# Merging the block inverses of the four DeltaNet heads in lockstep: four visits of small matmuls instead of sixteen

## The chip, the cores and the metric

The kernel runs on one core of a Trainium2 chip. The metric is the device time of one execution in microseconds (us). The engines of a core work side by side, each through its own instructions in order: TensorE (PE, matmuls, with the weight load PEld in front of each), VectorE (DVE), ScalarE (ACT), GpSimd (POOL), and SyncE (SP), which issues DMAs.

## The reference

One layer of a decoder trunk, sequence 1024, width 1024, float32. One input projection feeds two mixers: a gated DeltaNet with 4 heads of 128 (causal convolution on q, k and v, normalised q and k, chunked delta rule) and a dilated sliding-window attention with 8 heads of 64. Both outputs go through one output projection and a residual; a gated MLP with a short convolution, another residual and a norm follow. The part that is touched is the triangular solve of the delta rule:

```python
lmat = dec_strict * kk * bc[..., None, :]
rhs = jnp.concatenate([vc, gam * kc], axis=-1)
sol = lax.linalg.triangular_solve(lmat, rhs, left_side=True, lower=True, unit_diagonal=True)
u_v, w_k = sol[..., :Dv], sol[..., Dv:]
```

## The kernel before

**The solve.** The kernel works with chunks of 128 tokens, so 8 chunks for each of 4 heads, and inverts the 128x128 unit triangular matrix of each. `kprep` builds the matrices of a head (tile um) and parks their diagonal 32x32 blocks in DRAM. When all heads are there, `forward_sub` (line 663) inverts all diagonal blocks of 32x32 (4 for each chunk and head) on VectorE, in 31 steps over all blocks at once, and parks the inverses and their transposes (xdram, xtdram). `merge` (line 698) then puts larger inverses together from smaller ones: for a lower triangular matrix in 2x2 blocks, the block below the diagonal of the inverse is minus (one inverse) times (the block) times (the other inverse), so two products. From 32 to 64 these are the products into w1p and y1p (32x32 matmuls), from 64 to 128 those into w2p and y2p (64x64). Between two products the result is copied from PSUM to SBUF by ACT and DVE. Each matmul on float32 stands in the trace as two instructions.

**Before, pair by pair.** `merge` is a generator and runs once for each pair of heads, as a stream of its own (line 688). Each of the four products is cut into a part for each head (`for e in range(2)`), and `apart` (line 693) keeps the parts at least MGAP = 0.6 us from each other on the planner's clock, so that projection products stand between them: 2 pairs x 4 products x 2 heads = 16 visits. Pair 0 uses the PSUM tag "asc", pair 1 "ch", each with two banks.

**What sets the order.** The class `Weave` runs generators ("streams") with a level each; `wv.need(...)` gives the planned time at which a tile is ready, and a stream yields until then, with a slack (MSLACK = 1.5 us for the merges). The last argument of `mm` is what a matmul costs on the planner's clock of TensorE. Line 191 stamps every matmul with its place, so TensorE's order is the planner's. The order on the other engines is made by the framework's scheduler; the instructions of the recurrence go through `uv` and `ua`, which raise their priority.

**What stands around.** `dense` (line 505) is the stream of the lowest priority: 25 column tiles of the projection, each 2 x 24 products of 128x128 by 128x512 (tiles xhi, xlo, whi, wlo: three products for each of 8 slices of the width). Each half of 24 has a PSUM bank ("hf", two of them), which DVE evacuates (`scaled`, tile xr or aqkv). At each column tile the weights of the next one but one are loaded (wst), and those of the next are split by ACT (whi) and DVE (wlo). `chain` (line 791) is the recurrence over 8 chunks, once for each head; it begins when all four heads are merged (`wv.until(("m", i))`). One chunk takes the products ct,kT, then r,um, then wke,ktok, then ct,qat and w,qat, with DVE and ACT between them (r, wke, w, ct, vtok). Its tiles qat come by DMA from parked tensors; the loads for the second half of heads 0 and 1 use the same two slots ("go") as the tiles x64. The attention follows when the chains are done.

Of the kernel before, what the change touches and what calls it, by code (L numbers as in the profile page):

```python
# [7 lines left out]
F32 = mybir.dt.float32  # L8
F32R = mybir.dt.float32r
AF = mybir.ActivationFunctionType  # L10
OP = mybir.AluOpType
# [4 lines left out]
P = 128  # L16
S = 1024
KT = 8
H = 4
NCH = 8  # L20
# [16 lines left out]
MSLACK = 1.5  # L37
# [3 lines left out]
MGAP = 0.6  # L41
# [103 lines left out]
def hybrid_layer(tc, I, out):  # L145
    nc = tc.nc
    wv = Weave()
    ve = Engine(wv, nc.vector, "vector", 0.07, 0.00105)
    ac = Engine(wv, nc.scalar, "scalar", 0.12, 0.00085)
# [3 lines left out]
    po_ = Engine(wv, nc.gpsimd, "gpsimd", 0.15, 0.0021)  # L153
    sy = Engine(wv, nc.sync, "sync", 0.05, 0.00142, 2.2)
# [6 lines left out]
    sp = es.enter_context(tc.tile_pool(name="sp", bufs=1))  # L161
# [3 lines left out]
    def tile_(pool, shape, dt, name, tag, bufs):  # L165
        return wv.slot(pool.tile(list(shape), dt, name=name, tag=tag, bufs=bufs), tag, bufs)
# [20 lines left out]
    def after(inst, anchor, reason="keeps a slot free until it is needed"):  # L187
        tc.add_manual_dep(inst.ins, anchor.ins.name, order, reason=reason)

    def mm(dst, lhs, rhs, us, start=True, stop=True, **kw):  # L190
        tc.stamp_issue_order_token(nc.tensor.matmul(dst, lhs, rhs, start=start, stop=stop, **kw).ins, TOKEN)  # L191
        wv.product(us, dst, lhs, rhs)
# [52 lines left out]
    xdram = dp.tile([H, 32, 1024], F32, name="xdram")  # L245
    xtdram = dp.tile([H, 32, 1024], F32, name="xtdram")
# [6 lines left out]
    def bank(tag, name="ps"):  # L253
        return tile_(pp_, (P, 512), F32, name, tag, 2)
# [239 lines left out]
    G = [dict() for _ in range(H)]  # L494
# [82 lines left out]
    def kprep(h):  # L577
# [50 lines left out]
        if all(("k", i) in wv.done for i in range(H)):  # L628
            forward_sub()
# [33 lines left out]
    def forward_sub():  # L663

        mt_t = A("mt", "go")
        sy.dma_start(mt_t, mdram.rearrange("h p f -> (h p) f"))
        mt = mt_t.rearrange("p (j i) -> p j i", j=32)
        xi_t = A("xi", "go")
        xi = xi_t.rearrange("p (i c) -> p i c", i=32)
        tmp = tile_(sp, [P, 256], F32, "tmp", "t1", 1)  # L670
        po_.memset(xi, 0.0)
        po_.affine_select(xi, xi, pattern=[[1, 32], [-1, 32]], compare_op=OP.not_equal, fill=1.0, base=0,
                                channel_multiplier=0)

# [12 lines left out]
        for p in range(2):  # L687
            wv.add(2, merge(p, anchor))

    mlast = [0.0]  # L690
    mark = const("mark", [P, 1])

    def apart():

        while wv.pe < mlast[0] + MGAP:
            yield mlast[0] + MGAP - wv.pe

    def merge(pair, anchor):

        tag = ("asc", "ch")[pair]  # L700
        yield wv.need(xdram)
        hs2 = (2 * pair, 2 * pair + 1)
        yts = [G[h].pop("um") for h in hs2]
        x64 = A("x64", "go", shape=(P, 2, NCH, 64))
        after(po_.memset(x64, 0.0), anchor)
        xd = xdram[2 * pair:2 * pair + 2].rearrange("h (c r) (i j) -> r i (h c) j", r=4, i=32)
        for r in range(4):
            b, o = slice(32 * r, 32 * r + 32), 32 * (r % 2)
            sy.dma_start(x64[b, :, :, o:o + 32].rearrange("p h c j -> p (h c) j"), xd[r])
        for e in range(2):  # L710
            xtd = xtdram[hs2[e]].rearrange("(c r) (j i) -> r j c i", r=4, j=32)
            for r in range(4):
                b = slice(32 * r, 32 * r + 32)
                sy.dma_start(yts[e][b, :, b], xtd[r])

        halves = [(slice(64 * p, 64 * p + 32), slice(64 * p + 32, 64 * p + 64)) for p in range(2)]
        w1p = bank(tag)
        yield wv.need(w1p, x64, *yts)
        w1v = w1p.rearrange("p (h c j) -> p h c j", h=2, c=NCH)
        w1 = tile_(sp, [P, 2, NCH, 32], F32, "w1", "t2", 2)  # L720
        for e in range(2):
# [5 lines left out]
        for b, op in ((halves[0][1], True), (halves[1][1], False)):  # L727
            if op:
                ac.activation(w1[b], w1v[b], AF.Copy)
            else:  # L730
                ve.tensor_copy(w1[b], w1v[b])
        y1p = bank(tag)
        yield wv.need(y1p, w1, slack=MSLACK)
        y1v = y1p.rearrange("p (h c j) -> p h c j", h=2, c=NCH)
        for e in range(2):
            yield from apart()
            for c in range(NCH):
                for a, b in halves:
                    mm(y1v[a, e, c, :], w1[b, e, c, :], yts[e][b, c, b], 0.03)
                b = halves[0][1]  # L740
                mm(y1v[b, e, c, :], yts[e][b, c, b], w1[b, e, c, :], 0.03)
            mlast[0] = wv.pe
        for a, b in halves:
            for e in range(2):
                ac.activation(yts[e][a, :, b], y1v[a, e], AF.Copy, scale=-1.0)
        ve.tensor_scalar(x64[32:64, :, :, 0:32], y1v[32:64], -1.0, None, op0=OP.mult)
        if pair == 1:
            po_.tensor_copy(mark[32:33], x64[32:33, 0, 0, 0:1])

        lo, up = slice(0, 64), slice(64, 128)  # L750
        w2p = [bank(tag) for _ in range(2)]
        yield wv.need(*w2p, x64, *yts, slack=MSLACK)
        w2 = []
        for e in range(2):
            yield from apart()
            w2v = w2p[e].rearrange("p (c j) -> p c j", c=NCH)
            for c in range(NCH):
                mm(w2v[up, c, :], yts[e][lo, c, up], x64[lo, e, c, :], 0.11)
            mlast[0] = wv.pe
            w2.append(tile_(sp, [P, NCH, 64], F32, "w2", "t2", 2))  # L760
# [4 lines left out]
        for e in range(2):  # L765
            y2p = bank(tag)
            yield wv.need(y2p, w2[e], slack=MSLACK)
            yield from apart()
            y2v = y2p.rearrange("p (c j) -> p c j", c=NCH)
            for c in range(NCH):  # L770
                mm(y2v[lo, c, :], w2[e][up, c, :], yts[e][up, c, up], 0.11)
            mlast[0] = wv.pe
            if e == 0:
                ac.activation(yts[e][lo, :, up], y2v[lo], AF.Copy, scale=-1.0)
            else:
                ve.tensor_scalar(yts[e][lo, :, up], y2v[lo], -1.0, None, op0=OP.mult)
            G[hs2[e]]["yt"] = yts[e]
            wv.done.add(("m", hs2[e]))

    def chain_load(h, s):  # L780
        t = A("qat", "go" if s == 1 and h < 2 else "qa", shape=(P, 2, 512))
# [985 lines left out]
```

## Time and profile before

| | us |
|---|---|
| time, median of 3 runs (lowest, highest) | 1205.56 (1205.49, 1207.72) |
| span of the profiled execution, first to last instruction | 1204.1 |
| around the span, median less span | 1.46 |
| TensorE busy in the span | 1194.7 |
| stretch with the merges, first product with x64 to last with w2 | 191.7 to 225.5 |

Times in the profile are counted from the first instruction of the span. A row of the timeline gives start, length, engine, line, operation, tiles (out<-in), shapes and the number of instructions in a row; in brackets the idle time of the engine before it and what ended it. Matmuls overlap: one of 0.39 us starts 0.23 us after the one before, so starts are compared, not lengths. All products carry line 191, that of the helper, so they are told apart by tiles: ps<-xhi,whi is a product of the projection, ps<-x,um (x64 is shown as x) and ps<-um,w those of the merges.

### The profile page before, as it was taken

Reading aid. Unit: us, or ns where it says so; the run is one execution under the profiler, and the core shown is the slowest. Engines: PE = TensorE matmul, PEld = TensorE weight load, DVE = VectorE, ACT = ScalarE, POOL = GpSimd, SP = SyncE. Lnnn points to the kernel's source line nnn. Section 1 sums busy time; section 2 is a strip of 40 time slices with the busy share of each in tenths; the row PEclk is TensorE's granted clock in tenths of the full one; section 3 lists DMA queues with packets and bytes.
Section 4 is the critical chain, followed back from the end, with each engine's and each line's share of the span. In section 5 each row is a group of like instructions: output and inputs, shape, how many; then the busy total and the mean of one; then the engine's idle time right before and its main releaser. Section 6 shows DMA issues by size and latency. Waiting matters only on the chain.

```text
span 1204.1 us, 18360 instructions
## 1 busy us (share of the span) xinstructions
PE 1194.7 (99%) x7058; PEld 987.9 (82%) x7058; DVE 957.1 (79%) x1530; ACT 575.9 (48%) x1131; POOL 54.3 (5%) x50
## 2 busy tenths in 40 slices
PE   9999999999999999999999999999999999999997
PEld 7888887898777777888888888888888888888887
DVE  7686985474667687767898989889898889898987
ACT  7383344364444444555554544444454454445452
POOL 0212110023000000000000000000000000000001
PEclk9999999999999999999999999999999999999999
DMA  7323234426433323443123132231322296357734
GB/s 236 106 75 102 77 119 122 157 79 212 166 115 106 106 63 123 150 140 140 56 85 106 59 100 89 69 105 53 105 71 86 94 370 227 109 179 223 242 97 157
DMA packets 81704, 152.72 MB, mean 127 GB/s; under 512 B 21552, under 2 KB 32592, under 8 KB 81616
## 3 DMA queue, kind: packets, MB, share of 16 engines
q1 hardware_dynamic: 80896, 151.02, 38.3%
q8 instruction: 55, 0.90, 0.3%
q10 hardware_dynamic: 720, 0.53, 0.1%
q14 instruction: 33, 0.27, 0.1%
HBM read 113.49 MB, written 35.93 MB: 124 GB/s over the span
## 4 chain that ended last, share of the span: by engine, by line
PE 98%; DVE 1%; ACT 0%; issue 0%; POOL 0%; DVEq 0%; ACTq 0%; POOLq 0%
PE ps L191 48%; PE pa L191 20%; PE dw L191 17%; PE pc L191 10%; PE ps L195 2%; PE ps L200 1%; PE warm L191 0%; DVE x1h L139 0%; ACT sm L141 0%; PE pd L191 0%; DVE sm L141 0%; POOL rs L139 0%; DVE xr L139 0%; ACT u L139 0%; ACT sq L139 0%
## 5 line engine op out<-in xcount | busy, mean ns | idle before, releaser
L191 PE MATMUL dw<-pr 128*128 128x512 f32 (+1 forms) x984 | 211.4, 377 | 0.0
L191 PEld LDWEIGHTS dw<-pr 128*128 128x128 f32 x984 | 176.8, 188 | 33.5
L191 PE MATMUL ps<-xhi,whi 128*128 128x512 f32 x448 | 186.4, 416 | 0.0
L191 PE MATMUL ps<-xhi,wlo 128*128 128x512 f32 x448 | 175.8, 392 | 0.0
L191 PE MATMUL ps<-xlo,whi 128*128 128x512 f32 x448 | 175.4, 391 | 0.0
L191 PE MATMUL pa<-T,pair 128*128 128x512 f32 x528 | 127.1, 390 | 0.1
L191 PEld LDWEIGHTS pa<-T,pair 128*128 128x128 f32 x528 | 99.0, 188 | 20.9 <-ACT u L139 0.5
L191 PEld LDWEIGHTS ps<-xhi,whi 128*128 128x128 f32 x448 | 84.7, 189 | 19.4 <-issue 2.7
L191 PEld LDWEIGHTS ps<-xhi,wlo 128*128 128x128 f32 x448 | 84.3, 188 | 18.4
L191 PEld LDWEIGHTS ps<-xlo,whi 128*128 128x128 f32 x448 | 84.9, 189 | 13.7
L139 ACT ACTIVATE u<-pa 128x512 f32<-128x512 f32 x44 | 26.3, 599 | 109.7 <-PE pa L191 109.7
L139 DVE SCALAR_TENSOR_TENSOR y<-xu,fcw,y 128x1023 f32<-128x1023 f32 (+1 forms) x44 | 56.4, 1281 | 24.4 <-ACT y L139 24.4
L139 ACT ACTIVATE pr<-wd 128x1024 fp32r<-128x1024 f32 x33 | 35.0, 1061 | 73.9 <-DVE wd L139 36.9
L139 ACT ACTIVATE whi<-wst 128x1024 fp32r<-128x1024 f32 (+2 forms) x38 | 38.6, 1015 | 62.7 <-PE ps L191 55.7
L191 PE MATMUL pa<-B,A 128*128 128x512 f32 x264 | 63.5, 390 | 0.0
L191 PE MATMUL pa<-T,S 128*128 128x512 f32 x264 | 63.4, 390 | 0.0
L191 PE MATMUL pc<-T,S 128*128 128x512 f32 x264 | 63.4, 390 | 0.0
L191 PE MATMUL pc<-B,pair 128*128 128x512 f32 x264 | 63.4, 390 | 0.0
L139 DVE TENSOR_TENSOR wst<-wst 128x512 f32<-128x512 f32 x88 | 60.5, 687 | 0.8
L191 PE MATMUL ps<-B,pair 128*128 128x512 f32 x252 | 60.6, 390 | 0.0
L141 ACT ACTIVATE sm<-sm,mx 128x128 f32<-128x128 f32 (+7 forms) x64 | 35.5, 555 | 48.1 <-DVE mx L141 48.1
L191 PEld LDWEIGHTS pa<-T,S 128*128 128x128 f32 x264 | 49.6, 188 | 10.2
(240 smaller groups left out, 2253.1 us busy)
## 6 DMA issues: line engine op xcount, KB each, us to landing
wst<-in_wu SPq DMA_DIRECT2D x44, 512.0 KB, 3.7
wd<-in_wd SPq DMA_DIRECT2D x44, 512.0 KB, 4.5
wst<-in_wi SPq DMA_DIRECT2D x25, 512.0 KB, 3.7
upark<-y SPq DMA_DIRECT2D x22, 512.0 KB, 3.7
r<-upark SPq DMA_DIRECT2D x22, 512.0 KB, 10.2
apark<-aqkv SPq DMA_DIRECT2D x12, 512.0 KB, 3.0
wa<-in_wd SPq DMA_DIRECT2D x22, 256.0 KB, 3.0
wst<-in_wo SPq DMA_DIRECT2D x8, 512.0 KB, 3.8
```

Of the source, the lines that this page charges most:

```text
L139: return getattr(eng, op)(*a, **kw)
L141: return getattr(eng, op)(*a, **kw)
L191: tc.stamp_issue_order_token(nc.tensor.matmul(dst, lhs, rhs, start=start, stop=stop, **kw).ins, TOKEN)
L195: tc.stamp_issue_order_token(nc.tensor.transpose(dst, src, ident).ins, TOKEN)
L200: tc.stamp_issue_order_token(nc.tensor.transpose(dst, src[rows], ident[rows, rows]).ins, TOKEN)
```

## The change

`merges` takes the place of `merge`: one stream for all four heads. Each of the four products is made for the four heads in one go, with nothing of the planner between (`apart` and MGAP's use are gone), so there are four visits, and each waits for the tiles of all four heads. Both PSUM tags are used at once. The planner's costs of the small matmuls are lower (0.03 to 0.02 or 0.01; 0.11 to 0.067). Of the copies after the second product one in four goes from ACT to DVE. The third product's result goes into the upper half of x64, which is free by then, in place of a tile w2 of its own. The matmuls themselves are the same in number, shapes and operands.

```diff
-        for p in range(2):
-            wv.add(2, merge(p, anchor))
+        wv.add(2, merges(anchor))
...
-        w1p = bank(tag)
-        yield wv.need(w1p, x64, *yts)
-        for e in range(2):
-            yield from apart()
+        w1ps = [bank(t) for t in tags]
+        yield wv.need(*w1ps, *x64s, *ys)
+        for h, y, x64, e in heads:
             for c in range(NCH):
                 for a, b in halves:
-                    mm(w1v[b, e, c, :], yts[e][a, c, b], x64[a, e, c, 0:32], 0.03)
-            mlast[0] = wv.pe
+                    mm(four(w1ps[h // 2])[b, e, c, :], y[a, c, b], x64[a, e, c, 0:32], 0.02)
...
+        y1ps = [bank(t) for t in tags]
+        yield wv.need(*y1ps, *w1s, slack=MSLACK)
+        for h, y, x64, e in heads:
+            w1, y1v = w1s[h // 2], four(y1ps[h // 2])
             for c in range(NCH):
                 for a, b in halves:
+                    mm(y1v[a, e, c, :], w1[b, e, c, :], y[b, c, b], 0.01)
                 b = halves[0][1]
+                mm(y1v[b, e, c, :], y[b, c, b], w1[b, e, c, :], 0.02)
+        for pair in range(2):
+            x64, y1v = x64s[pair], four(y1ps[pair])
+            ve.tensor_scalar(x64[32:64, :, :, 0:32], y1v[32:64], -1.0, None, op0=OP.mult)
...
+                    if (i, e) == (1, 1):
+                        ve.tensor_scalar(y[a, :, b], y1v[a, e], -1.0, None, op0=OP.mult)
+                    else:
+                        ac.activation(y[a, :, b], y1v[a, e], AF.Copy, scale=-1.0)
...
+        w2ps = [bank(t) for t in tags for _ in range(2)]
+        yield wv.need(*w2ps, *x64s, *ys, slack=MSLACK)
+        for h, y, x64, e in heads:
             for c in range(NCH):
-                mm(w2v[up, c, :], yts[e][lo, c, up], x64[lo, e, c, :], 0.11)
+                mm(w2vs[h][up, c, :], y[lo, c, up], x64[lo, e, c, :], 0.067)
+        for h, y, x64, e in heads:
             if e == 0:
-                ac.activation(w2[e][up], w2v[up], AF.Copy)
+                ac.activation(x64[up, e], w2vs[h][up], AF.Copy)
             else:
-                ve.tensor_copy(w2[e][up], w2v[up])
+                ve.tensor_copy(x64[up, e], w2vs[h][up])
+        y2ps = [bank(t) for t in tags for _ in range(2)]
+        yield wv.need(*y2ps, *x64s, slack=MSLACK)
+        for h, y, x64, e in heads:
             for c in range(NCH):
-                mm(y2v[lo, c, :], w2[e][up, c, :], yts[e][up, c, up], 0.11)
+                mm(y2v[lo, c, :], x64[up, e, c, :], y[up, c, up], 0.067)
```

More of the change, by code (lines that the diff above doesn't have):

```diff
@@ new lines, in merges, with four @@
+    def merges(anchor):
+        tags = ("asc", "ch")
+        yield wv.need(xdram)
+        ys = [G[h].pop("um") for h in range(H)]
+        x64s = []
+        for pair in range(2):
+            x64 = A("x64", "go", shape=(P, 2, NCH, 64))
+            x64s.append(x64)
+            after(po_.memset(x64, 0.0), anchor)
+            xd = xdram[2 * pair:2 * pair + 2].rearrange("h (c r) (i j) -> r i (h c) j", r=4, i=32)
+            for r in range(4):
+                b, o = slice(32 * r, 32 * r + 32), 32 * (r % 2)
+                sy.dma_start(x64[b, :, :, o:o + 32].rearrange("p h c j -> p (h c) j"), xd[r])
+            for h in (2 * pair, 2 * pair + 1):
+                xtd = xtdram[h].rearrange("(c r) (j i) -> r j c i", r=4, j=32)
+                for r in range(4):
+                    b = slice(32 * r, 32 * r + 32)
+                    sy.dma_start(ys[h][b, :, b], xtd[r])
+        heads = [(h, ys[h], x64s[h // 2], h % 2) for h in range(H)]
+        halves = [(slice(64 * p, 64 * p + 32), slice(64 * p + 32, 64 * p + 64)) for p in range(2)]
+        def four(t):
+            return t.rearrange("p (h c j) -> p h c j", h=2, c=NCH)
+        w1ps = [bank(t) for t in tags]
+        yield wv.need(*w1ps, *x64s, *ys)
+        for h, y, x64, e in heads:
@@ L723, in merge @@
             for c in range(NCH):
                 for a, b in halves:
-                    mm(w1v[b, e, c, :], yts[e][a, c, b], x64[a, e, c, 0:32], 0.03)
-            mlast[0] = wv.pe
[L727 to L734, printed above, removed]
@@ L735, in merge @@
-        for e in range(2):
-            yield from apart()
+                    mm(four(w1ps[h // 2])[b, e, c, :], y[a, c, b], x64[a, e, c, 0:32], 0.02)
+        w1s = []
+        for p in w1ps:
+            w1 = tile_(sp, [P, 2, NCH, 32], F32, "w1", "t2", 2)
+            w1s.append(w1)
+            ac.activation(w1[halves[0][1]], four(p)[halves[0][1]], AF.Copy)
+            ve.tensor_copy(w1[halves[1][1]], four(p)[halves[1][1]])
+        y1ps = [bank(t) for t in tags]
+        yield wv.need(*y1ps, *w1s, slack=MSLACK)
@@ L746, in merge @@
-        ve.tensor_scalar(x64[32:64, :, :, 0:32], y1v[32:64], -1.0, None, op0=OP.mult)
-        if pair == 1:
-            po_.tensor_copy(mark[32:33], x64[32:33, 0, 0, 0:1])
-        lo, up = slice(0, 64), slice(64, 128)
[L751 to L756, printed above, removed]
+                mm(y1v[b, e, c, :], y[b, c, b], w1[b, e, c, :], 0.02)
@@ new lines, in merges @@
+        for pair in range(2):
+            x64, y1v = x64s[pair], four(y1ps[pair])
+            ve.tensor_scalar(x64[32:64, :, :, 0:32], y1v[32:64], -1.0, None, op0=OP.mult)
+            if pair == 1:
+                po_.tensor_copy(mark[32:33], x64[32:33, 0, 0, 0:1])
+            for i, (a, b) in enumerate(halves):
+                for e in range(2):
+                    y = ys[2 * pair + e]
+                    if (i, e) == (1, 1):
+                        ve.tensor_scalar(y[a, :, b], y1v[a, e], -1.0, None, op0=OP.mult)
+                    else:
+                        ac.activation(y[a, :, b], y1v[a, e], AF.Copy, scale=-1.0)
@@ L757, in merge @@
+        lo, up = slice(0, 64), slice(64, 128)
+        w2ps = [bank(t) for t in tags for _ in range(2)]
+        yield wv.need(*w2ps, *x64s, *ys, slack=MSLACK)
+        w2vs = [p.rearrange("p (c j) -> p c j", c=NCH) for p in w2ps]
+        for h, y, x64, e in heads:
             for c in range(NCH):
-                mm(w2v[up, c, :], yts[e][lo, c, up], x64[lo, e, c, :], 0.11)
-            mlast[0] = wv.pe
-            w2.append(tile_(sp, [P, NCH, 64], F32, "w2", "t2", 2))
+                mm(w2vs[h][up, c, :], y[lo, c, up], x64[lo, e, c, :], 0.067)
@@ L761, in merge @@
+        for h, y, x64, e in heads:
             if e == 0:
-                ac.activation(w2[e][up], w2v[up], AF.Copy)
+                ac.activation(x64[up, e], w2vs[h][up], AF.Copy)
             else:
-                ve.tensor_copy(w2[e][up], w2v[up])
[L765 to L769, printed above, removed]
+                ve.tensor_copy(x64[up, e], w2vs[h][up])
@@ L770, in merge @@
+        y2ps = [bank(t) for t in tags for _ in range(2)]
+        yield wv.need(*y2ps, *x64s, slack=MSLACK)
+        for h, y, x64, e in heads:
+            y2v = y2ps[h].rearrange("p (c j) -> p c j", c=NCH)
             for c in range(NCH):
-                mm(y2v[lo, c, :], w2[e][up, c, :], yts[e][up, c, up], 0.11)
-            mlast[0] = wv.pe
+                mm(y2v[lo, c, :], x64[up, e, c, :], y[up, c, up], 0.067)
+        for h, y, x64, e in heads:
+            y2v = y2ps[h].rearrange("p (c j) -> p c j", c=NCH)
@@ L773, in merge @@
             if e == 0:
-                ac.activation(yts[e][lo, :, up], y2v[lo], AF.Copy, scale=-1.0)
+                ac.activation(y[lo, :, up], y2v[lo], AF.Copy, scale=-1.0)
             else:
-                ve.tensor_scalar(yts[e][lo, :, up], y2v[lo], -1.0, None, op0=OP.mult)
-            G[hs2[e]]["yt"] = yts[e]
-            wv.done.add(("m", hs2[e]))
+                ve.tensor_scalar(y[lo, :, up], y2v[lo], -1.0, None, op0=OP.mult)
+            G[h]["yt"] = y
+            wv.done.add(("m", h))
```

26 lines of the change are left out of this document (removed).

## The prediction

> **What bounds the kernel now.** I read the page first (busy time, the chain that ended last), then the timeline of TensorE around the block inverses, then the same stretch on ScalarE and VectorE, and beside them the order of each engine's instructions in the built programs of both versions.
>
> ```profile
> span 1204.1 us, 18360 instructions
> PE 1194.7 (99%) x7058; PEld 987.9 (82%) x7058; DVE 957.1 (79%) x1530; ACT 575.9 (48%) x1131; POOL 54.3 (5%) x50
> PE 98%; DVE 1%; ACT 0%; issue 0%; POOL 0%; DVEq 0%; ACTq 0%; POOLq 0%
> L191 PE MATMUL ps<-wke,ktok 128*128 128x128 f32 x56 | 10.7, 281 | 0.5 <-ACT w L141 0.5
> ```
>
> TensorE (PE) is busy 99% of the span and makes up 98% of the chain. Its idle time inside the stretch that matters is 0.5 us, at one product of the recurrence. So its time is the sum of the distances from one matmul's start to the next, and a change counts by what it does to those distances. Any wait that it adds on PE counts in full.
>
> Starts on PE around the merges (timeline: start, length, instruction):
>
> ```profile
> 188.46 0.39 PE L191 MATMUL ps<-xhi,wlo 128*128 128x512 f32 x1
> 188.69 0.39 PE L191 MATMUL ps<-xhi,whi 128*128 128x512 f32 x1
> 188.91 0.39 PE L191 MATMUL ps<-xlo,whi 128*128 128x512 f32 x1
> ...
> 190.05 1.03 PE L195 MATMUL ps<-ident,qT 128*128 128x128 f32 x8
> ...
> 192.34 0.50 PE L191 MATMUL ps<-xhi,whi 128*128 128x512 f32 x1
> 192.67 0.39 PE L191 MATMUL ps<-xlo,whi 128*128 128x512 f32 x1
> 192.91 0.40 PE L191 MATMUL ps<-xhi,wlo 128*128 128x512 f32 x1
> 193.23 0.69 PE L191 MATMUL ps<-x,um 32*32 32x32 f32 x32
> 193.85 0.50 PE L191 MATMUL ps<-xhi,whi 128*128 128x512 f32 x1
> ...
> 202.82 0.19 PE L191 MATMUL ps<-w,um 32*32 32x32 f32 x1
> 202.95 0.51 PE L191 MATMUL ps<-xhi,whi 128*128 128x512 f32 x1
> ...
> 209.25 1.14 PE L191 MATMUL ps<-x,um 64*64 64x64 f32 x16
> 210.32 0.50 PE L191 MATMUL ps<-xhi,whi 128*128 128x512 f32 x1
> ...
> 226.15 0.48 PE L191 MATMUL ps<-xhi,whi 128*128 128x512 f32 x1
> 226.93 0.38 PE L191 MATMUL ps<-vtok,um 128*128 128x128 f32 x2
> ...
> 227.85 1.05 PE L191 MATMUL ps<-wke,ktok 128*128 128x128 f32 x8
> ```
>
> Projection products alone start every 0.23 us (188.46, 188.69, 188.91). A triple of them between two visits of small matmuls takes 193.23 - 192.34 = 0.89 us where three pitches would be 0.68: going into and out of small matmuls costs **0.21 us per visit**. The visit has a tail too. The 32 instructions at 193.23 end at 193.92. One lasts 0.19 (the rows grouped by form have 192 ns), so the last starts at 193.73, 0.12 before the next product; inside the visit they follow every 0.016. The tail of the products with w1 is 202.95 - 202.82 = 0.13, of the 64-wide ones 0.15 (210.32 less 210.39 - 0.22), against 0.01 and 0.06 from one to the next inside.
>
> **The change part by part.** The number of matmuls stays what it was, and so does the kind of each; the instruction order on PE is the same up to the query transposes at 190.05 and again, but for the places of projection products, from the first wke product on.
>
> Visits. Sixteen become four. Twelve entries and exits go: 12 x 0.21 = 2.5 us. Twelve tails go, three of the first kind, three of the second and six 64-wide: 3 x (0.12 - 0.016) + 3 x (0.13 - 0.01) + 6 x (0.15 - 0.06) = 1.2 us. The first products of the recurrence (vtok,um) are no longer split by a triple, which took 226.93 - 226.15 = 0.78 instead of 0.68: 0.1 us. Sum of the gain: **3.8 us**.
>
> Place. From 190.05 to 227.85 before has 72 projection products, after 90. The chain of the recurrence opens 15 products later in the order (18 less 3 that now do not stand behind the first wke), which is 3.4 us of products, less the 3.8 gained: 0.4 us earlier on the clock. Those 15 products go from a stretch near the end of the attention, where 42 products now stand around one turning of probabilities because it has to wait for the projection. The planner's sequence is otherwise kept, so I count nothing there.
>
> Waits that the merged visits could bring. All loads are issued in the old order. Evacuations before:
>
> ```profile
> 186.91 3.94 SPq L139 DMA_DIRECT2D um<-xtdram  x8
> DMA to landing us min/median/max: 1.5/1.9/3.4
> 201.54 0.59 ACT L139 ACTIVATE w<-ps 32x512 f32<-32x512 f32 x1 [1.81 <-PE ps L191]
> 204.61 1.29 ACT L139 ACTIVATE um<-ps 32x256 f32<-32x256 f32 x4 [2.48 <-PE ps L191]
> 207.39 2.17 ACT L141 ACTIVATE vtok<-ps,nk 128x128 f32<-128x128 f32 x8 [1.49 <-PE ps L195]
> 202.16 0.70 DVE L139 COPY w<-ps 32x512 f32<-32x512 f32 x1 [0.20 <-ACT w L139]
> 205.93 0.68 DVE L139 TENSOR_SCALAR x<-ps 32x512 f32<-32x512 f32 x1 [3.07 <-ACT um L139]
> 212.39 0.69 DVE L139 COPY w<-ps 64x512 f32<-64x512 f32 x1 [1.00 <-PE ps L191]
> ```
>
> The last load is issued by 190.9 and lands by 194.3; the first merged visit comes at 199.0 (190.05 plus 27 products and three small groups). Its 128 instructions take 2.2 us. ScalarE (ACT) copies pair 0 when half are done and pair 1 by 201.8, VectorE (DVE) waits for ACT on the same tile, as in the row at 202.16, and ends by 202.5; the y1 visit comes 18 products on, at 205.5: 3 us to spare. After y1 (ends 207.6), DVE and ACT alternate: x64 0.7, three um copies 1.0, um 0.4 for pair 0, done by 208.7; then ACT has the eight vtok (2.2) ahead of pair 1's um copies, which end at 211.5, the last um on DVE at 211.9. The w2 visit starts at 212.7 with pair 0 and reaches pair 1 at 214.7: 2.8 us to spare. Between w2 and y2 there are four copies, two on each engine, 0.7 each (as at 212.39), done 0.8 us after w2 ends, with 18 products as cover. After y2 (ends 225.1) the last um ends at 225.9 and is read at 227.2. So the merges themselves add **no wait**; if a cover of 18 products (4.1 us) were gone, each visit would wait for 1 to 4 us. x64 now also takes w2's place, so its slot comes free 3 to 4 us later, and two loads of the chain, issued by SP, wait for it; they serve its fifth chunk, over 10 us on.
>
> Where a stall comes in. The 15 products shift the projection's own VectorE work, the evacuation aqkv and the split wlo, into the recurrence:
>
> ```profile
> 227.62 0.39 PE L191 MATMUL ps<-xhi,wlo 128*128 128x512 f32 x1
> 239.58 0.40 PE L191 MATMUL ps<-xhi,wlo 128*128 128x512 f32 x1
> 239.81 0.39 PE L191 MATMUL ps<-wke,ktok 128*128 128x128 f32 x2
> 240.71 0.42 PE L191 MATMUL ps<-ct,kT 128*128 128x128 f32 x2
> 228.05 1.07 DVE L139 TENSOR_TENSOR aqkv<-ps,rstdB 128x512 f32<-128x512 f32 x1 [0.34 <-PE ps L191]
> 228.96 0.87 DVE L141 COPY ct<-ps 128x128 f32<-128x128 f32 x4
> 236.31 1.23 DVE L139 TENSOR_TENSOR wlo<-wst,whi 128x1024 fp32r<-128x1024 f32 x1
> 240.24 0.35 DVE L141 SCALAR_TENSOR_TENSOR ct<-ct,ge,ps 128x128 f32<-128x128 f32 x1 [0.57 <-PE ps L191]
> 264.55 1.08 DVE L139 TENSOR_TENSOR aqkv<-ps,rstdB 128x512 f32<-128x512 f32 x1
> 271.31 0.42 PE L191 MATMUL ps<-ct,kT 128*128 128x128 f32 x2
> ```
>
> Before, no aqkv stands on DVE between 235 and 264.5, while PE runs the recurrence with few projection products between. There the loop is tight: wke,ktok at 239.81, its state update on DVE 240.24 to 240.59, ct,kT at 240.71. After, the 24th product of a bank is the one at 239.58 and the program puts its aqkv ahead of that update. It starts 0.43 after the product (as 228.05 after 227.62) at 240.0, the next instruction follows 0.91 later (228.96 after 228.05), so the update runs from 240.9, and ct,kT starts 0.7 late. Between nothing (were DVE to slip it into a hole) and its whole 1.07 I take **0.7**. The next bank and weight boundary falls at the product that now starts at 268.35: the same sum puts aqkv, wke and r on DVE until 270.2, then wlo, so that the update before the ct,kT at 271.31 ends 0.4 late, and ACT's split of the weights delays a copy by 0.1. Between nothing and 1.23 I take **0.5**. Further boundaries fall where six to nine products stand between two steps of the recurrence: nothing. In the attention both versions put aqkv and wlo mostly ahead of the softmax; nothing, with 1.1 (one aqkv) as the upper end. Below nothing: the 0.5 us at wke,ktok may go.
>
> **Sum.** 3.8 - 0.7 - 0.5 = 2.6 us off the span: 1201.5. The median 1205.56 is 1.46 above the profiled span, for start and end around it, which the change does not touch: 1201.5 + 1.46 = **1202.9 us**.
>
> **The rivals.**
> *No stall in the recurrence* (DVE hides it, as it hid the wlo at 236.31 there with hardly a delay): 1205.6 - 3.8 = 1201.8. Against it stands the loop without slack at 240.71. Chance 0.27.
> *DVE costs more*: aqkv, wlo at their whole lengths and one more aqkv in the attention, 1.07 + 1.23 + 1.1 = 3.4: 1205.2, within 0.2%. Chance 0.25 for all between 1203.6 and 1208.
> *Slower: the recurrence takes every shifted piece at full price.* After has four aqkv and two wlo on DVE between the chain's first r and its end. If PE has to wait out each, 4 x 1.07 + 2 x 1.23 = 6.7 outweighs 3.8: 1208.5. It decides from about 6.2 us of such stalls. Against it: the aqkv at 264.55 stands in the recurrence too, and no idle time of PE is listed behind it. Chance 0.05.
> *Slower: the clock.* A merged 64-wide visit keeps PE on quarter-size matmuls for 64 x 0.062 = 4.0 us; were that taken for idleness and the clock halved, 18 products behind each of two such visits would take 4.1 us longer: 1202.9 + 8.2 = 1211.1.
>
> ```profile
> 201.50:209.20 7.70, 7.70 (x215) 5.64 (x215) 1.85 (x3) 3.68 (x13) 0.00 (x0) 1.00 0.08 28
> 1199.00:1204.00 5.00, 0.00 (x0) 0.00 (x0) 1.30 (x4) 0.00 (x0) 1.01 (x2) 0.50 0.64 210
> ```
>
> The sixth figure after the length is PE's granted clock, followed by DMA. With four visits in 7.7 us it stays at 1.00; only where PE has no instruction at all is it 0.50. Chance 0.02. [...]
> *That the change does not do what it says* is excluded by the program's order: four visits, 18 products between each two.
>
> **How the numbers follow.** The forecast, 1202.3 to 1203.6, has 0.41. 0.2% (2.4 us, about what a measurement of this kernel can tell from no change) lies at 1203.15 and cuts it: seven tenths of it are faster. Faster 0.27 + 0.29 = 0.56, within 0.2% 0.12 + 0.25 = 0.37, slower 0.07. Range: from 1201.3 (no stall and the 0.5 gone) to 1205.2 (the second rival).
>
> **What would show it.** Right: four groups of small matmuls of 2.2, 2.2, 4.0 and 4.0 us, the projection products between them 0.23 apart, no idle on PE ahead of them; the first wke,ktok near 228.2 with 18 more products done; in the recurrence one ct,kT 0.7 and a later one 0.5 us behind, each with aqkv or wlo on DVE before it. Wrong: idle on PE at the y1, w2 or y2 visit (an evacuation late); visits longer than their instructions make them; a clock under 1.00; or stalls at the turning of probabilities in the attention.

## The result, and the profile after

| | median (lowest to highest), us | span of the profiled execution, us |
|---|---|---|
| before | 1205.59 (1205.13 to 1207.72), 12 runs | 1204.1 |
| after | 1203.20 (1202.57 to 1205.16), 12 runs | 1200.8 |

The ratio is 0.9979, 95% interval 0.9971 to 0.9987: 2.4 us less (1.6 to 3.5). The forecast was 1202.9.

The rows of the page and of the grouped answer for 188 to 305 us, after (columns as before: busy, mean ns | idle time and what ended it):

```profile
span 1200.8 us, 18366 instructions
PE 1190.4 (99%) x7058; PEld 986.1 (82%) x7058; DVE 956.5 (80%) x1532; ACT 575.3 (48%) x1129; POOL 57.1 (5%) x50
L191 PE MATMUL ps<-wke,ktok 128*128 128x128 f32 x56 | 10.7, 281 | 0.5 <-ACT w L141 0.5
L191 PE MATMUL ps<-ct,kT 128*128 128x128 f32 x56 | 10.6, 285 | 0.6 <-DVE ct L141 0.6
```

TensorE has the same 7058 instructions and is 4.3 us less busy; the 0.5 us at wke,ktok stand, and 0.6 us at ct,kT are new. The visits, in TensorE's timeline after:

```profile
189.22 1.03 PE L195 MATMUL ps<-ident,qT 128*128 128x128 f32 x8
...
198.13 2.21 PE L191 MATMUL ps<-x,um 32*32 32x32 f32 x128
200.27 0.50 PE L191 MATMUL ps<-xhi,whi 128*128 128x512 f32 x1
...
204.57 0.22 PE L191 MATMUL ps<-um,w 32*32 32x32 f32 x2
...
206.84 1.09 PE L195 MATMUL ps<-ident,vT 128*128 128x128 f32 x8
...
211.97 3.94 PE L191 MATMUL ps<-x,um 64*64 64x64 f32 x64
215.85 0.50 PE L191 MATMUL ps<-xhi,whi 128*128 128x512 f32 x1
...
220.15 3.94 PE L191 MATMUL ps<-um,x 64*64 64x64 f32 x64
224.03 0.50 PE L191 MATMUL ps<-xhi,whi 128*128 128x512 f32 x1
...
227.11 1.05 PE L191 MATMUL ps<-wke,ktok 128*128 128x128 f32 x8
```

From the start of a visit to the next instruction: 2.14, 2.27, 3.88 and 3.88 us, with no bracket, so no idle time ahead of any. Over these stretches the granted clock stays at 1.00 (a row of such a table: length, busy time and instructions of PE, PEld, DVE, ACT and POOL, then the clock, the DMA share, GB/s):

```profile
198.13:200.27 2.14, 2.14 (x129) 2.10 (x129) 1.17 (x2) 0.59 (x1) 0.00 (x0) 1.00 0.66 257
211.97:215.85 3.88, 3.88 (x66) 3.81 (x65) 1.69 (x2) 1.18 (x2) 0.00 (x0) 1.00 0.96 326
```

Where time came from and went shows best in three stretches, each less its projection products at 0.2275 us (their mean pitch inside long rows of them, in both timelines), because the versions have different numbers of them in each stretch. **Visits**: from the query transposes (190.05 before, 189.22 after) to the first wke,ktok (227.85, 227.11). **Recurrence**: from there to the last ct,kT. **Attention**: from there to the first product of the MLP. Before, the visits are 227.85 - 190.05 = 37.8 us with 72 products, so 21.4; after, 37.9 us with 90, so 17.4.

The rows below the first two are the experiments told further on; "earlier" is the place in TensorE's order at which the recurrence opens, against after.

| | visits | recurrence | attention | median, us |
|---|---|---|---|---|
| before | 21.41 | 35.41 | 160.27 | 1205.6 |
| after | 17.42 | 36.35 | 160.76 | 1203.2 |
| 1: sixteen visits, place of after | 21.41 | 36.35 | 160.77 | 1207.05 |
| 2: four visits, 15 products earlier | 17.75 | 35.59 | 160.29 | 1202.0 |
| 4: aqkv moved back | 17.48 | 36.17 | 160.72 | 1203.25 |
| 6: 9 products earlier | 17.53 | 35.95 | 160.68 | 1202.8 |
| 7: 21 products earlier | 17.44 | 36.47 | 160.54 | 1203.4 |
| 8: 18 products earlier | 17.44 | 36.45 | 160.61 | 1203.5 |
| 10: as 2, wke first | 17.53 | 35.36 | 160.32 | 1201.7 |

The change takes 3.99 us out of the visits and gives back 0.94 in the recurrence and 0.49 in the attention: 2.56. The span fell by 3.3, because this execution also started 0.83 us faster (189.22 for 190.05, with the same instructions up to there; in the other profiles of this study that start lies anywhere from 189.2 to 190.1), so the change's part of it is the 2.56.

What was given back, on TensorE and VectorE in the recurrence:

```profile
238.93 0.39 PE L191 MATMUL ps<-r,um 128*128 128x128 f32 x2
239.73 0.49 PE L191 MATMUL ps<-ct,kT 128*128 128x128 f32 x2 [0.42 <-DVE ct L141]
...
270.22 0.39 PE L191 MATMUL ps<-r,um 128*128 128x128 f32 x2
270.79 0.49 PE L191 MATMUL ps<-ct,kT 128*128 128x128 f32 x2 [0.18 <-DVE ct L141]
```

```profile
238.46 1.05 DVE L139 TENSOR_TENSOR aqkv<-ps,rstdB 128x512 f32<-128x512 f32 x1 [0.24 <-PE ps L191]
239.36 0.32 DVE L141 SCALAR_TENSOR_TENSOR ct<-ct,ge,ps 128x128 f32<-128x128 f32 x1
...
269.25 1.22 DVE L139 TENSOR_TENSOR wlo<-wst,whi 128x1024 fp32r<-128x1024 f32 x1
270.38 0.35 DVE L141 SCALAR_TENSOR_TENSOR ct<-ct,ge,ps 128x128 f32<-128x128 f32 x1
```

Elsewhere ct,kT starts 0.22 us after r,um; here 0.80 and 0.57. In both places the update it reads (ct) stands on VectorE right behind an aqkv or a wlo, and begins 0.90 us after the start of the aqkv and 1.13 after that of the wlo. In the attention it is the same, with the scaling of the probabilities:

```profile
366.45 1.07 DVE L139 TENSOR_TENSOR aqkv<-ps,rstdB 128x512 f32<-128x512 f32 x1
367.35 0.40 DVE L141 TENSOR_SCALAR sm<-sm,mx 128x384 f32<-128x384 f32 x1
```

```profile
367.24 1.30 PE L200 MATMUL ps<-ident,sm 64*128 64x64 f32 x24
```

These 24 transposes took 0.96 us before (at 367.75) and take 1.30: the second half waits for the scaled probabilities, behind an aqkv that came earlier before. Such a wait inside a row carries no bracket; the row's length tells it.

### The profile page after: what moved, and what is told of

Read it like the earlier page. It is cut to its first block, busy times and chain, and to the rows that moved or that the text cites. A ratio compares the mean times of both kernels' runs of the same rounds, so it can differ in the third digit from the quotient of the medians.

```text
span 1200.8 us, 18366 instructions
## 1 busy us (share of the span) xinstructions
PE 1190.4 (99%) x7058; PEld 986.1 (82%) x7058; DVE 956.5 (80%) x1532; ACT 575.3 (48%) x1129; POOL 57.1 (5%) x50
## 4 chain that ended last, share of the span: by engine, by line
PE 96%; DVE 2%; ACT 1%; DMA 1%; issue 0%; POOL 0%; DVEq 0%; SPq 0%; ACTq 0%; POOLq 0%
PE ps L191 46%; PE pa L191 20%; PE dw L191 17%; PE pc L191 10%; PE ps L195 2%; PE ps L200 1%; DMA wst<-in_wu 0%; ACT sm L141 0%; DVE x1h L139 0%; DMA xt<-in_xT 0%; DVE sm L141 0%; DVE aqkv L139 0%; DVE T L139 0%; DVE wst L139 0%; DVE pair L139 0%
## 5 line engine op out<-in xcount | busy, mean ns | idle before, releaser
L191 PEld LDWEIGHTS pc<-B,pair 128*128 128x128 f32 x264 | 49.6, 188 | 10.3
```

## The experiments

Theory: a visit costs what its entry, exit and tail cost, whatever else moves; the shift of the recurrence by 15 products costs what an evacuation of the projection (aqkv) or a weight split (wlo) delays on VectorE. Rivals: the gain came from the moved products; the merges themselves wait; the clock.

### Two by two: number of visits, place of the recurrence

**1, sixteen visits at the late place.** In each of the four products, between two heads (`apart` as before the change):

```diff
-MSLACK = 1.5
+MSLACK = -1.06
...
         for h, y, x64, e in heads:
+            yield from apart()
             for c in range(NCH):
...
+            mlast[0] = wv.pe
```

> The changed kernel with each of its four visits cut into its four heads again, three projection products between two heads, and fewer products between the visits (6, 9, 6 in place of 18, 18, 18), so that the recurrence opens behind the same product and TensorE's and VectorE's order from there on is the changed kernel's. Theory (entering and leaving small matmuls costs 0.21 us, a tail 0.1): twelve more visits cost 3.7 to 4.0 us, so 1206.9 to 1207.2 against 1203.2, slower than the kernel before; each triple between two heads lasts 0.89 us; the stalls of 0.5 and 0.4 us at ct,kT in the recurrence stay. Rival (the 15 products that moved made the gain, not the visits): 1203.2, within 0.5.

Measured: 1207.05 us (ratio to before 1.0008, 1.0000 to 1.0017). The whole 3.99 us of the visits are back, to 0.01, and recurrence and attention are the changed kernel's to 0.01. A triple between two heads:

```profile
198.75 0.50 PE L191 MATMUL ps<-xhi,whi 128*128 128x512 f32 x1
...
199.64 0.69 PE L191 MATMUL ps<-x,um 32*32 32x32 f32 x32
```

199.64 - 198.75 = 0.89 us for 0.68 us of products. Twelve visits for 3.99 us: 0.33 us each. The rival of the moved products falls.

**2, four visits at the early place.**

```diff
-        yield wv.need(*y1ps, *w1s, slack=MSLACK)
+        yield wv.need(*y1ps, *w1s, slack=0.2)
...
-        yield wv.need(*w2ps, *x64s, *ys, slack=MSLACK)
+        yield wv.need(*w2ps, *x64s, *ys, slack=0.4)
...
-        yield wv.need(*y2ps, *x64s, slack=MSLACK)
+        yield wv.need(*y2ps, *x64s, slack=0.4)
```

> The changed kernel with fewer products between its four visits (12, 12, 15 in place of 18, 18, 18), so that the recurrence opens behind the product behind which it opened before the change; TensorE's and VectorE's order from there on is that of the kernel before. Theory (visits 4.0 us less; the shift by 15 products costs 0.9 us in the recurrence and 0.6 in the attention): no idle time at ct,kT, 4.0 us below the kernel before, 1201.6, and 1.6 below the changed one. Rival (these stalls come from the merges, or from chance, not from the place): 1203.2, with ct,kT late as before. If twelve products are too little cover, idle time shows on TensorE at the second or third visit.

Measured: 1202.0 us (0.9967, 0.9955 to 0.9979). Attention as before the change, no idle time at ct,kT: what was given back belongs to the place, not to the merges. Of the 4.0 us expected against before 3.7 came, because at this place an aqkv stands ahead of the four first wke on VectorE. They begin 1.12 us after the vtok,um products (222.83) that they follow, where experiment 10, without that aqkv in front, has 0.42: 0.7 us late, which delays wke,ktok by 0.2:

```profile
223.03 1.10 DVE L139 TENSOR_TENSOR aqkv<-ps,rstdB 128x512 f32<-128x512 f32 x1 [0.91 <-PE ps L191]
223.95 1.10 DVE L141 TENSOR_SCALAR wke<-ps,ke 128x128 f32<-128x128 f32 x4
```

### What the place costs

**4, the aqkv ahead of the late ct,kT, six instructions further back on VectorE.**

```diff
+    def behind(inst):
+        if state:
+            after(inst, state[-1], "the recurrence goes first")
...
-                ve.tensor_tensor(t[:, sl].rearrange("p (n c u) -> p n u c", n=4, c=4),
+                inst = ve.tensor_tensor(t[:, sl].rearrange("p (n c u) -> p n u c", n=4, c=4),
...
+                behind(inst)
...
-                    uv.scalar_tensor_tensor(sn, st, ge[:, c:c + 1], ps[:, 2 * P:3 * P], op0=OP.mult, op1=OP.add)
+                    state.append(uv.scalar_tensor_tensor(sn, st, ge[:, c:c + 1], ps[:, 2 * P:3 * P], op0=OP.mult, op1=OP.add))
```

(`behind` is called for wlo too, whose place it leaves.)

> The changed kernel with one evacuation aqkv, the one ahead of the late ct,kT, moved six instructions back on VectorE, behind the next three ct updates. Theory A (it costs because it stands ahead of the update that ct,kT waits for): the idle 0.42 us at ct,kT goes and none takes its place: 0.5 us less, 1202.7. Theory B (VectorE has no hole there that holds 0.9 us): the idle time shows up again, 0.3 to 0.6 us at a wke,ktok or ct,kT within the next 3 us, and the time stays within 0.3 of 1203.2. The time alone can hardly tell 0.5 us; the idle time on TensorE in the profile does.

Measured: 1203.25 us, and in the recurrence 0.18 us less.

```profile
239.90 0.39 PE L191 MATMUL ps<-r,um 128*128 128x128 f32 x2
240.12 0.42 PE L191 MATMUL ps<-ct,kT 128*128 128x128 f32 x2
...
243.21 0.40 PE L191 MATMUL ps<-xhi,wlo 128*128 128x512 f32 x1
243.71 0.49 PE L191 MATMUL ps<-wke,ktok 128*128 128x128 f32 x2
```

ct,kT follows r,um by 0.22 again, so the cause is shown; but a wke,ktok 3.6 us on starts 0.50 after the product ahead of it instead of 0.23. Theory B, nearly: VectorE has no hole there for 0.9 us, and the delay moves.

**6, 7, 8, other places** (15, 12, 15; 12, 9, 12; 12, 12, 12 products between the visits: MSLACK = 0.85, then 0.2, then 0.2, 0.4, 0.2 in the lines of experiment 2).

> The changed kernel with 15, 12 and 15 products between its visits, so that the recurrence opens 9 products earlier in the order than in the changed kernel (45). Theory (the place only decides which step of the recurrence and of the attention an evacuation delays): the four visits take 2.14, 2.26, 3.87, 3.87 us as before, the idle time at ct,kT moves or goes, and the time lies between 1201.3 (the second experiment less its 0.7 us of late wke and w1) and 1203.2. Rival (the earlier the recurrence opens the better, 1.2 us for 15 products): 1202.5.

> The changed kernel with 12, 9 and 12 products between its visits: the recurrence opens 21 products earlier than in the changed kernel (33 products). Theory (place by place): visits as in the changed kernel, idle time by where the evacuations fall, 1201.3 to 1203.2. Rival (the earlier the better, 0.08 us a product): 1201.5.

> The changed kernel with 12, 12 and 12 products between its visits: the recurrence opens 18 products earlier than in the changed kernel, 3 earlier than in the second experiment. Theory (place by place): 1201.3 to 1203.2; if the evacuation that delayed the first wke copies in the second experiment stands elsewhere, wke,ktok loses none of its 0.5 us. Rival (the earlier the better): 1201.7.

Measured: 1202.8, 1203.4 and 1203.5 us (ratios 0.9974, 0.9982, 0.9981, each with about 0.0009 to both sides). The visits stay at 17.4 to 17.5. The recurrence lies between 35.95 and 36.47, the attention between 160.5 and 160.7, in no order of earlier or later: the eighth opens 18 products before the changed kernel and takes 1203.5, where the rival wanted 1201.7 (the interval reaches down to 1202.2). Place by place holds. The three times differ by less than their intervals; the stretches, of one execution each, carry this reading.

**10, the early place with that aqkv behind the first wke.**

```diff
+                if len(firsts) == H:
+                    after(inst, firsts.pop(), "the recurrence opens first")
...
-                uv.tensor_scalar(wke, ps[:, P:2 * P], ke[:, c:c + 1], None, op0=OP.mult)
+                inst = uv.tensor_scalar(wke, ps[:, P:2 * P], ke[:, c:c + 1], None, op0=OP.mult)
+                if c == 0:
+                    firsts.append(inst)
```

> The second experiment's kernel (1202.0) with the one evacuation aqkv that stands ahead of the four first wke copies on VectorE put behind them. Theory (an evacuation costs what it delays): wke,ktok opens 0.23 us earlier and is not split, 0.4 to 0.5 us less, 1201.5 to 1201.6, and aqkv delays none of the ct copies behind it by more than 0.9 us, which the 15 products there cover. Rival (the delay only moves to the ct copies and to the products that read them): 1202.0.

Measured: 1201.7 us (0.9968, 0.9955 to 0.9980), 3.75 below before in the same comparison. Experiment 2 is 3.7 below before in its own, so the times do not tell these two apart; the stretches, of one execution each, do.

```profile
222.94 1.13 DVE L141 TENSOR_SCALAR wke<-ps,ke 128x128 f32<-128x128 f32 x4 [1.13 <-PE ps L191]
223.99 1.05 DVE L139 TENSOR_TENSOR aqkv<-ps,rstdB 128x512 f32<-128x512 f32 x1
224.87 0.87 DVE L141 COPY ct<-ps 128x128 f32<-128x128 f32 x4
```

The three stretches are 0.42 us shorter together than in experiment 2, as the theory wanted. With 15 products behind it, the ct copy can wait.

### How much cover, and the clock

**3, no product between the visits.**

```diff
-MSLACK = 1.5
+MSLACK = -2.6
```

> The changed kernel with no projection product between the four visits. The prediction said that without its cover each of the three later visits would wait 1 to 4 us: 3 to 12 us more, less three entries and exits (0.9): 1205 to 1214. Rival, from the trace of the changed kernel (a copy of the first pair is done 0.5 us after the first visit, the six um copies and their pair 1.2 us after the second, and the 64-wide copies of a head while the next heads are multiplied): waits of 0.5, 1.2 and 0 us, less 0.9, so 1203 to 1205, with about 1 us either way for the new place of the recurrence.

Measured: 1214.5 us (1.0069, 1.0057 to 1.0082). The waits are the rival's and less, 0.41 us for a copy and 0.62 that nothing released ("issue"). The visits' stretch, though, is 7.7 us longer than after's (25.15 for 17.42; the recurrence, which opens 57 products earlier, is 1.6 longer, the attention 0.8), and that is the clock:

```profile
200.91 0.21 PE L191 MATMUL ps<-um,w 32*32 32x32 f32 x1 [0.41 <-DVE w L139]
202.85 0.18 PE L191 MATMUL ps<-w,um 32*32 32x32 f32 x1 [0.62 <-issue]
```

```profile
203.00:207.00 4.00, 4.00 (x118) 3.94 (x111) 1.10 (x2) 2.50 (x7) 0.36 (x2) 0.57 0.15 52
207.00:212.00 5.00, 5.00 (x53) 5.00 (x53) 1.72 (x3) 0.59 (x1) 0.00 (x0) 0.50 0.49 155
```

It falls to 0.50 at about 203.5 (a mean of 0.57 over the four us means 0.56 us of full clock in them), and the two 64-wide visits take 6.8 and 6.6 us instead of 3.9 each. The fourth rival of the prediction exists, though not in the changed kernel, whose four visits have 1.00.

**5, three products between the visits** (MSLACK = -1.9).

> The changed kernel with three projection products (0.7 us) between each two visits in place of 18. By the changed kernel's trace the copies that the next visit's first head needs end 0.5, 1.2 and 0 us after a visit, and the value transposes stand before the third visit, so that TensorE should wait 0.3 us in all. Theory A (the clock is halved only when products over the whole array are missing for more than about 5 us at a stretch; with none between the visits it fell 5.3 us after the last of them): each stretch without them is at most 3.9 us, the granted clock stays at 1.00, and the time is 1201 to 1203.5, by where the recurrence then falls. Theory B (a share of full products over a longer time counts, and 0.7 us between visits of 2 to 4 us is too little): the clock falls to 0.50 at the third or fourth visit and these take twice their 3.9 us: 1205 to 1212.

Measured: 1203.1 us (0.9976, 0.9967 to 0.9986), theory A's side: the clock stays at 1.00, and one wait of 0.44 us ("issue") is all there is.

```profile
202.00:204.00 2.00, 1.56 (x138) 1.51 (x126) 0.68 (x1) 0.78 (x3) 0.00 (x0) 1.00 0.39 130
```

**9, the 64-wide visits back to back** (slack=-5.0 in the last of the lines of experiment 2, MSLACK elsewhere).

> The changed kernel with no projection product between the third and the fourth visit (18, 18 and 0 in place of 18, 18, 18), so that 7.75 us of 64-wide matmuls follow each other without idle time on TensorE; the recurrence opens where it does in the eighth experiment (1203.5), with the same order from there. Theory A (full products missing for 5.3 us halve the clock): the last 2.4 us of the two visits take twice as long, and some 1.4 us more are lost until the clock is back, less one entry and exit of 0.3: 1206 to 1208, and the granted clock is 0.50 at the end of the fourth visit. Rival (in the third experiment it was the 1.0 us of idle TensorE in between that let the clock fall): the clock stays at 1.00, 1203.2.

Measured: 1202.4 us (0.9976, 0.9967 to 0.9985). Theory A falls: 7.4 us of 64-wide matmuls (212.23 to 219.66) without a full product leave the clock where it is. (The 0.8 us under the rival's 1203.2 are in part the visit that was saved: 17.02 for 17.44.)

```profile
216.00:218.00 2.00, 2.00 (x41) 2.00 (x38) 0.80 (x2) 0.59 (x1) 0.00 (x0) 1.00 0.92 230
218.00:219.00 1.00, 1.00 (x21) 1.00 (x20) 0.58 (x1) 0.17 (x1) 0.00 (x0) 1.00 0.86 344
```

**11, the first visit three times over.**

```diff
-        for h, y, x64, e in heads:
+        for h, y, x64, e in heads * 3:
             for c in range(NCH):
                 for a, b in halves:
                     mm(four(w1ps[h // 2])[b, e, c, :], y[a, c, b], x64[a, e, c, 0:32], 0.02)
```

> The changed kernel with the first visit's 64 products with x64 made three times over into the same places (the same values again): 384 instructions, 6.4 us of 32-wide matmuls with no idle time on TensorE between them, and the recurrence at the changed kernel's place. What is open is what let the clock fall in the third experiment and not in the ninth. Theory (32-wide matmuls, which fill a sixteenth of the array, do not count as work, 64-wide ones do): the granted clock falls about 5.3 us after the last full product, the last 1.1 us take twice as long and about 1.4 us more pass until it is back: 4.3 us for the instructions and 2.5 on top, 1210. Rival (idle TensorE is needed, 1.0 us of it stood in the third experiment): the clock stays at 1.00, the 4.3 us alone, 1207.5, give or take 0.5.

Measured: 1212.3 us (1.0045, 1.0031 to 1.0059), 9.1 above the changed kernel. The premise failed: idle time came by itself.

```profile
198.76 3.85 PE L191 MATMUL ps<-x,um 32*32 32x32 f32 x231
203.38 2.21 PE L191 MATMUL ps<-x,um 32*32 32x32 f32 x128 [0.77 <-issue]
207.11 0.85 PE L191 MATMUL ps<-x,um 32*32 32x32 f32 x25 [1.52 <-issue]
```

```profile
206.00:207.00 1.00, 0.00 (x0) 0.00 (x0) 0.33 (x1) 0.00 (x0) 0.00 (x0) 0.64 0.00 0
```

The clock outlasts 6.8 us of 32-wide matmuls (198.76 to 205.59) with a pause of 0.77 in them, and falls at about 206.3, inside the second pause (0.64 over that us). The theory's 5.3 us, which would be 204.0, is wrong; the last section has what the traces show in its place.

**12, no product between the first two visits alone** (slack=-5.0 in the first of the lines of experiment 2).

> The changed kernel with no projection product between the first and the second visit alone (0, 18 and 18), which leaves 5.5 us without a full product, with 1.0 us of idle TensorE in it, as in the third experiment; the recurrence opens where it does in the eighth (1203.5) with the same order from there. Theory (such a stretch, 32-wide and with the idle time, lets the clock fall 5.3 us after the last full product): the wait of 1.0 us, less 0.3 for an entry and exit, and 0.5 to 1.5 us at half the clock behind it: 1204.7 to 1205.7, with the granted clock under 1.00 behind the second visit. Rival (the clock needs more than one such stretch, or fell for the 64-wide visits that followed at once): the wait alone, 1203.0 to 1204.2, the clock at 1.00.

Measured: 1207.8 us (1.0012, 1.0004 to 1.0021), 4.2 above the eighth, which has the same order behind it; 3.0 of that are in the visits' stretch (20.47 for 17.44), the rest in the MLP (last section). The pauses are 0.41 (the copy) and 1.1 ("issue"), and the clock is at 0.50 from 204.0 to about 207.4. Pauses of 1.46 and 3.4 us at half the clock (1.7 us of work lost), less an entry and exit of 0.3, make 2.8 of the 3.0. The theory wanted 1.2 to 2.2: the clock fell as it said, but both the pause and the time at half clock were longer. The rival falls.

```profile
204.00:207.00 3.00, 3.00 (x63) 2.54 (x53) 1.36 (x3) 1.06 (x4) 0.36 (x2) 0.50 0.03 10
207.00:209.00 2.00, 2.00 (x12) 1.78 (x11) 0.17 (x1) 1.60 (x7) 0.00 (x0) 0.91 0.94 184
```

## Why the prediction was right

Point by point, by its own steps.

- **Visits, 3.8 us**: measured 3.99, and shown by experiment 1 to be the visits alone. The entry, exit and tail that one row gave (0.21 and about 0.1) are 0.33 together.
- **Place, first wke,ktok near 228.2 with 18 more products done**: it came at 227.11, or 227.94 with the start's 0.83 put back. Right, by the 0.2 that the visits gave more.
- **No wait at the merged visits**: right. The last w1 copy ends at 201.7, 2.9 us ahead of the second visit (3 were predicted).
- **What a lost cover would cost, 1 to 4 us a visit**: this step failed. With three products instead of 18 (experiment 5) no visit waits for a copy, since the copies of the first pair are done while the second pair is multiplied; with none one visit waits 0.41. Cover has another use that the prediction did not see: with three products TensorE was idle for 0.44 us and the clock stayed at 1.00, with none it was idle for 1.02 and the clock fell to 0.50.
- **Stalls in the recurrence, 0.7 and 0.5 us**: there, at the two products that were named, behind the aqkv and the wlo that were named, with 0.58 and 0.35 (0.80 and 0.57 less 0.22). Together with smaller shifts the recurrence lost 0.94 where 1.2 was forecast. Experiments 2 and 4 show the cause: at another place, or behind another instruction, ct,kT is on time.
- **Nothing in the attention**: this step failed by 0.49, within the 1.1 that it named as the upper end; a stall at the turning of the probabilities was one of its own signs of being wrong. For 0.34 of it, one aqkv fell between the reciprocal and the scaling of the probabilities. The planner's sequence was kept, as I wrote, but the same evacuation met another step of it.
- **Sum 2.6 us, time 1202.9**: the three stretches give 2.56, and the median 2.4. The two misses (0.26 too much in the recurrence, 0.49 too little in the attention) and the 0.2 at the visits cancel: that the sum is right to 0.04 is luck, that its parts are right to half a microsecond is not.

The rivals: no stall (1201.8) fell with the 0.6 us at ct,kT. DVE costs more (1205.2) had the right three places, with the one in the attention that the forecast left out, but they cost 0.58, 0.35 and 0.34, 1.3 us in all and not 3.4. All shifted pieces at full price (1208.5) fell: of four aqkv and two wlo in the recurrence, one of each is seen to delay TensorE, by about a half and a third of its length. The clock (1211.1) did not come here, at 1.00 in all four visits, nor in 7.4 us of 64-wide matmuls in a row (experiment 9), and did at the merges of experiments 3, 11 and 12. In the 3.41 us before each of these falls TensorE was idle for 1.0 to 1.5 us, among 32-wide matmuls without a full product.

## What to carry to other kernels

When TensorE is the bound, count how often it changes between full products and small matmuls, not only the matmuls: here each such visit cost 0.33 us, and grouping gave it back in full. Then look at what the regrouping shifts: another engine's long instruction (0.9 us here) that lands in front of a short one on a tight loop takes back a third of the gain, and moving the place by a few products, or that one instruction, wins it again (1203.2 to 1201.7). Keep a few full products between groups of small matmuls even where no copy needs the time (1203.1 us with three, 1214.5 with none).

## What the runs showed of the hardware

- **Pauses without a releaser in long rows of small matmuls.** At a pitch of 0.016 us TensorE paused after about 230 instructions of the merges in experiments 3, 5, 11 and 12 (0.44 to 1.1 us, "issue"), and in experiment 11 again 128 instructions later, for 1.52. With 18 products ahead of the second visit there is none. My reading, the supply of instructions, is an estimate from the counts below; no run changes that supply, so it is not shown. The pause comes at the same place in TensorE's program in all four kernels, after its 1240th matmul instruction (1242nd in 11). And the page has a queue for instructions, here that of experiment 11, with a row of the stretch between its two pauses (last figures: DMA share, GB/s):

```profile
q8 instruction: 57, 0.93, 0.3%
204.00:205.00 1.00, 1.00 (x76) 1.00 (x70) 0.00 (x0) 0.00 (x0) 0.00 (x0) 1.00 0.08 16
```

That run has 14628 instructions of PE and PEld to the 57 transfers; the changed kernel, with 256 matmuls and their weight loads less, has 14116 to 55. An estimate from these counts is 257 instructions to one transfer, so about 128 matmuls with their weight loads: the distance of the two pauses. In the row, 16 GB/s over one us are one transfer of 16 KB. By the trace's DMA records it starts at 204.63, the one before at 201.03, and the pauses end 2.48 and 2.35 us later. In that time 128 matmuls at 0.016 us (2.1 us) are used up, while 18 products at 0.2275 last 4.1 us.

- **The clock was at half for 3.41 us or a multiple of it.** At the merges it was at 0.50 for 3.41 us (experiment 12: 203.96 to 207.37), 6.83 (11) and 17.07 (3): once, twice and five times 3.41. Two stretches of this length before the fall of experiment 11, and one behind it:

```profile
199.45:202.86 3.41, 3.16 (x199) 3.05 (x194) 0.20 (x1) 0.00 (x0) 0.00 (x0) 1.00 0.47 171
202.87:206.28 3.41, 2.21 (x128) 2.10 (x128) 0.65 (x1) 0.59 (x1) 0.00 (x0) 1.00 0.23 71
206.28:209.69 3.41, 2.58 (x29) 2.21 (x29) 0.75 (x2) 0.59 (x1) 0.00 (x0) 0.50 0.02 7
```

In the first, 32-wide matmuls alone with 0.25 us idle (3.41 - 3.16), the clock stayed at 1.00, as in the second, which has 1.20 idle; it fell at the end of the second. The 3.41 us before the falls of 3 and 12 have 1.02 and 1.46 us idle and no full product either. In experiment 9 it stayed at 1.00 through 7.4 us of 64-wide matmuls alone without idle time, and in 5 with 0.44 us idle and three full products between the visits. So neither 32-wide nor 64-wide matmuls without a full product were seen to bring the clock down by themselves here; with 1.0 us of idle time among 32-wide ones it fell. For idle times between 0.25 and 1.02 us among 32-wide matmuls alone there is no run.

- **The clock in the MLP.** Some executions are 2 us longer: two of the twelve after the change take 1205.1 and 1205.2, at a mean granted clock of 0.996, the other ten 1202.6 to 1203.3 at 0.997 or 0.998. In the profiles of experiments 4, 6 and 12 the MLP takes 645.9 to 646.3 us, in the other eleven 643.9 to 644.8. In that of 4 the clock is at 0.50 for 3.41 us of it:

```profile
567.05:570.46 3.41, 3.17 (x23) 2.84 (x22) 3.28 (x6) 1.97 (x4) 0.00 (x0) 1.00 0.01 5
570.46:573.87 3.41, 3.41 (x10) 2.63 (x9) 3.41 (x7) 1.73 (x3) 1.95 (x1) 0.50 0.00 0
```

Ahead of the fall stand 16 matmuls with one column each (ps<-ones,rstdB, 1.84 us) and a wait of 0.24 us, with full products on both sides; TensorE is busy for 3.17 of the 3.41 us. All the kernels have these 16 matmuls, 10.2 us after the first product of the MLP. In the profile after the change they start at 566.83, with 0.13 us idle behind them, and the clock stays at 1.00. What decides between the two no run here shows.
